# Two thirds of a condition projection on VectorE instead of TensorE, in a two-block model on one core

## The chip, the core and the metric

The kernel runs on one core of one Trainium2 chip. The metric is the device time of one execution in microseconds (us). The engines are named as in the profile: PE is TensorE's matrix multiply and PEld its weight load, DVE is VectorE, ACT is ScalarE, POOL is GpSimd, SP is the engine whose queue issues most of the transfers.

## The reference, cut to what matters

The model has two parts. The first is two layers of a hybrid mixer (two attentions and a gated short convolution) and a feed-forward part, on 256 tokens of 1024 features. The second takes the result through an mLSTM mixer, a mixture of experts, a retention mixer and again a mixture of experts; its norms are modulated by two conditions, `c` for the 256 tokens and `c_ctx` for a context of 256 tokens more:

```python
for i in range(DEPTH):                     # DEPTH is 2
    mod_l = jnp.split(c_lat @ ada_w[i] + ada_b[i], N_MOD, axis=-1)   # ada_w[i]: [1024, 6144]
    mod_c = jnp.split(c_con @ ada_w[i] + ada_b[i], N_MOD, axis=-1)
    h_lat = modulate(rmsnorm(x, norm_mix_g[i]), mod_l[0], mod_l[1])
    h_ctx = modulate(rmsnorm(ctx, norm_mix_g[i]), mod_c[0], mod_c[1])
    ...
```

`c_lat` and `c_con` are silu of the two conditions. The condition projection depends on nothing that the first part computes, only its results are needed in the second part. In the last layer the context's results are needed for the mixer alone.

## The kernel before

All weights are float32 and come through one stream of chunks, 128 partitions by 2048 columns (1 MB), in the order of their use; SP issues their loads (`load`, L409). Four tiles take the raw chunks in turn. A chunk of a projection is split into two parts for TensorE: ACT copies its high part (`split`, L421), DVE forms its low part as raw minus high (L422), in two halves of 1024 columns each. Three pairs of tiles hold the parts. A product of two float32 operands is then three matmuls (`mm3`, L473 to L475: high by high, low by high, high by low). A column chunk of a projection is 48 such matmuls of 256 columns.

The plan of the stream (`stream_plan`) puts the 48 chunks of the condition projection (`"ada"`, 24 for each layer of the second part) into the first part of the model: 4 at the end of each mixer and of each feed-forward part (16 in all; `layer_norm` emits them, L887), and 32 spread over the rest of the first part, one about every third or fourth chunk. An `ada` chunk isn't split: `ada_chunk` (L494) multiplies it in 8 float32 matmuls by the two conditions, which stand as narrow columns in `csil`, over four groups of array columns; the four chunks of a group are added into `part` (ACT L500 for the first, DVE L502 for the others), and `ada_finish` turns a group with two matmuls (L510) and adds the bias (DVE L514) into `modc`, where every gain, shift and gate of the second part is read from. That makes 12 groups.

`parts(key)` is how every product gets its chunk: it first calls `run_ada`, which emits the condition chunks that stand next in the stream, and then `get`, which starts loads so that two chunks stand ready behind the one in use. A scheduler sets the order of each engine's instructions ahead of the run; every engine then runs its own list in order, so an instruction that waits holds up all behind it.

The first part's mixer (`mixer`) takes its projections in the order cq, ck, cv, aq, akv (L778 to L802), works through 8 tiles of two heads in `attention_pair` (scores L736 on PE, L740 to L750 on DVE, exp L752 and L753 on ACT, L758 to L760 on DVE, transposes L763 on PE, then the product with the values, L767 and L768), while PE also works on the convolution's projections (bc, bh, bb), then through 12 gate chunks with 6 branch chunks, and 4 output chunks. The feed-forward part (`ffn`) has 22 pairs of column tiles (g) and 11 chunks of the way down (d). `layer_norm` stands behind each; the rows for its gain and bias are loaded into two tiles with the tag `bc`.

Of the kernel before, what the change touches and what calls it, by code (L numbers as in the profile page):

```python
# [18 lines left out]
P = 128  # L19
T = 256  # L20
# [19 lines left out]
ADA_END = 4  # L40
NG = 4
# halves of chunks whose low parts GpSimd forms, VectorE being busy at that time
# [65 lines left out]
def stream_plan():  # L108
# [10 lines left out]
    # the ada chunks: some where the two blocks' parts meet, the others in between  # L119
    ada = [("ada", i, n) for i in range(LAYERS) for n in range(24)]  # L120
    spread = len(ada) - ADA_END * len(ends)
    free = [k for k in range(9, n1 - 4) if not any(e - 4 <= k <= e for e in ends)]
    mids = [free[len(free) * k // spread] for k in range(spread)]
    out = []
    for k, key in enumerate(plan):
        out.append(key)
        for _ in range(ADA_END * (k in ends) + mids.count(k)):
            out.append(ada.pop(0))
    assert not ada
# [16 lines left out]
def _pack(w):  # L146
    """[K, n] -> [P, (K / P, n)]"""
    k, n = w.shape
    return np.ascontiguousarray(w.reshape(k // P, P, n).transpose(1, 0, 2)).reshape(P, -1)


def _pack2(w):
    """[K, 2 n] -> [P, (2, K / P, n)]: a column half after the other."""
    n = w.shape[1] // 2
    return np.concatenate([_pack(w[:, :n]), _pack(w[:, n:])], axis=1)


def _chunk(key, x):
# [20 lines left out]
    if kind == "dn":  # L179
        return _pack(x["w_ffn_down"][key[1]][key[2] * 256 : key[2] * 256 + 256])  # L180
    if kind == "ada":
        return _pack(x["ada_w_2"][key[1]][:, key[2] * 256 : key[2] * 256 + 256])
# [26 lines left out]
# ---------------------------------------------------------------- small operands  # L209
# [58 lines left out]
def _rows(x):  # L268
# [6 lines left out]
    return np.stack(rows + [misc]).astype(np.float32)  # L275


def _constants():
# [23 lines left out]
    # distances of the keys (partition) from the queries: of the context backwards, of the latent stream backwards,  # L302
    # of the latent stream forwards (those past the key's tile first), of the context forwards
# [13 lines left out]
def kernel(  # L317
# [18 lines left out]
    # ------------------------------------------------------------ pools  # L336
# [17 lines left out]
    def bank(pool, tag, one=None):  # L354
        """The next of four banks in turn; one: False for one of the first three, True for the fourth."""
# [14 lines left out]
    # ------------------------------------------------------------ resident operands  # L370
# [21 lines left out]
    # ------------------------------------------------------------ weight stream  # L392
# [5 lines left out]
    def load(key, mid=None):  # L398
        """Start the load of the next chunk of the stream; mid: called between its halves."""
# [15 lines left out]
    def split(key, w, pair, half=None):  # L415
        """The float32r parts (hi, lo) of every 1024 columns of a chunk (or of one half), in the tiles of pair."""
# [9 lines left out]
    def load_parts(key):  # L426
        """Load the next chunk, as float32r parts."""
# [8 lines left out]
    def get(key, ahead=AHEAD):  # L436
        """The chunk of a key; the ones after it are started first."""
        while len(ready) < 1 + ahead and state["i"] < len(plan) and plan[state["i"]][0] != "moe":
            k = plan[state["i"]]
            ready.append((k, load(k) if k[0] == "ada" else load_parts(k)))  # L440
# [8 lines left out]
    def run_ada(end=False, rest=False):  # L449
        """The next ada chunks, and the ends of the last ones. At an end also the chunks behind those that are  # L450
        ready, their ends follow some chunks later; rest: all that is left."""
# [3 lines left out]
        while True:  # L455
            key = ready[0][0] if ready else None
            if key is None or key[0] != "ada":
# [13 lines left out]
    def mm3(o, st, mv, first, last):  # L471
        """o (+)= st^T mv in float32 from the parts (hi, lo) of both."""
# [4 lines left out]
    def warm(n):  # L477
        """Keep the tensor engine's clock up while a chain of short operations runs elsewhere."""
# [4 lines left out]
    # ------------------------------------------------------------ modulation  # L483
# [21 lines left out]

    def ada_finish():
# [16 lines left out]
    # ------------------------------------------------------------ small helpers  # L523
    def rsqrt(v, n, tag="nw"):
        """v ** -0.5 of a [P, n] tile by Newton's iteration."""
# [30 lines left out]
    def parts_of(pair, at, full):  # L556
        """pair[at] = parts of a float32 SBUF operand."""
# [10 lines left out]
    def evac_parts(ps, kp, dst, col0, gain, bias, direct=()):  # L568
        """dst (pair) [:, ko, col0 + 0:256] = parts of ps[:, k] * gain[ko] + bias[ko], ko = 2 kp + k."""
# [16 lines left out]
    def squares(ss, s, c, src, route=None):  # L586
        """ss [P, 2, streams, 4]: sums of squares of a column chunk, by token; route: whose scratch to use."""
# [8 lines left out]
    def rms_early(ss, n):  # L596
        """rms_rstd's share of all sums but the last."""
# [5 lines left out]
    def rms_rstd(ss, n, early=None):  # L603
        """1 / rms of every token, [P, n], from the sums of squares of some chunks [P, n, chunks]."""
# [4 lines left out]
    def diagonals(rs, n, pool, tag, bufs=1):  # L609
        """[P, n, P]: diagonal matrices of the columns of rs."""  # L610
# [5 lines left out]
    def normed(src, dg, dst, col0, gain, shift, bank=ax_bank, direct=()):  # L616
        """dst (pair) [:, ko, col0 + 0:256] = parts of (scaled src)^T * gain[ko] + shift[ko]; dg: by token tile."""
# [1559 lines left out]
```

## Time and profile before

| | |
|---|---|
| three runs | 2396.39 us median, 2392.59 to 2402.55 |
| profiled execution: span from the first to the last instruction | 2391.9 us (its own whole time is not given apart; the fastest run is 0.7 above the span, the median 4.5) |
| first part of the model | about 0 to 945 us of the span |
| PE busy | 2182.5 us (91%), 16939 instructions |
| DVE busy | 1093.7 us (46%), 2176 instructions |
| ACT busy | 737.6 us (31%) |
| chain of work that ended last | PE 65%, transfers 27%, DVE 6%, ACT 2% |
| granted TensorE clock over the span | 0.952 |

The page gives each engine's busy time over the whole span, and its share in 40 slices of the span, about 60 us each. An engine's average hides stages: the first part of the model is the first 16 slices, and the two mixtures of experts wait mostly for their weights. So the views used below are cut to stretches of the first part: 60 to 265 us is about the first layer's mixer (from its attention on), 265 to 460 its feed-forward part, 460 to 740 the second layer's mixer, 740 to 945 its feed-forward part. In the views, a row for a group of instructions has line, engine, operation, tiles and shapes, then the count, the busy time, the mean of one in ns, and the idle time ahead of them with what ended it.

### The profile page before, as it was taken

To read this page: it belongs to the slowest core of one execution; us is meant where nothing else is said; L and a number is where in the kernel's file an instruction comes from. 1 tells how busy PE (TensorE), PEld (TensorE's weight loads), DVE (VectorE), ACT (ScalarE), POOL (GpSimd) and SP (SyncE) were. 2 spreads that over 40 slices of the span, in tenths; PEclk is the share of its full clock that TensorE was granted. 3 is DMA by queue.
4 is the path that set the end of the run, shared out by engine and by line. 5 is a ranking of instruction groups with operands and counts; after the bars stand their busy time and mean duration, and the time that the engine had idled before them with its cause. 6 is when DMAs were issued, how large, how long until landed. Compare 5 with 4: busy or idle time off the path is not lost.

```text
span 2391.9 us, 39835 instructions
## 1 busy us (share of the span) xinstructions
PE 2182.5 (91%) x16939; PEld 1626.3 (68%) x16939; DVE 1093.7 (46%) x2176; ACT 737.6 (31%) x1353; POOL 76.3 (3%) x112
## 2 busy tenths in 40 slices
PE   8999999999999999999999999887899998766666
PEld 8799989897998998798885533222599874322222
DVE  5755744567567546765842222121573632010102
ACT  4543444345445444546521100000342521000000
POOL 0000000000000001201200000000110100000000
PEclk9999999999999999999999999999999999676777
DMA  7355666663557565122269999999743699999997
GB/s 297 129 189 229 257 240 233 240 221 122 211 216 299 212 236 186 71 106 71 81 272 360 408 372 421 421 421 421 298 152 107 229 365 420 421 421 421 421 420 294
DMA packets 92048, 652.40 MB, mean 273 GB/s; under 512 B 10336, under 2 KB 10592, under 8 KB 13920
## 3 DMA queue, kind: packets, MB, share of 16 engines
q1 hardware_dynamic: 89424, 641.61, 68.0%
q10 hardware_dynamic: 2448, 8.26, 1.0%
q8 instruction: 133, 2.18, 0.4%
q14 instruction: 43, 0.35, 0.0%
HBM read 648.78 MB, written 1.05 MB: 272 GB/s over the span
## 4 chain that ended last, share of the span: by engine, by line
PE 65%; DMA 27%; DVE 6%; ACT 2%; issue 1%; POOL 0%; ACTq 0%; SPq 0%; DVEq 0%; POOLq 0%
DMA w<-in_ws_dram 27%; PE mm L473 13%; PE mm L474 13%; PE mm L475 13%; PE mm L1726 5%; PE mm L1795 2%; PE mm L1220 2%; PE ax L473 2%; PE mm L494 2%; PE ax L475 2%; PE ax L1608 2%; PE ax L474 2%; PE ax L736 1%; PE ax L1815 1%; PE ax L623 1%
## 5 line engine op out<-in xcount | busy, mean ns | idle before, releaser
L422 DVE TENSOR_TENSOR lo<-w,hi 128x1024 fp32r<-128x1024 f32 x337 | 409.7, 1234 | 296.3 <-ACT hi L421 295.7
L421 ACT ACTIVATE hi<-w 128x1024 fp32r<-128x1024 f32 x343 | 352.3, 1053 | 462.8 <-PE mm L474 210.7
L1726 PE MATMUL mm<-w,xsT 128*32 128x256 f32 (+1 forms) x3072 | 404.2, 520 | 94.0 <-DMA w<-in_ws_dram 92.3
L473 PE MATMUL mm<-xTh,hi 128*128 128x256 f32 x1488 | 418.9, 282 | 6.5 <-ACT xTh L559 6.5
L474 PE MATMUL mm<-xTl,hi 128*128 128x256 f32 x1488 | 416.8, 280 | 1.5 <-DVE xTl L560 0.8
L475 PE MATMUL mm<-xTh,lo 128*128 128x256 f32 x1488 | 416.5, 280 | 0.0
L1726 PEld LDWEIGHTS mm<-w,xsT 128*32 128x32 f32 (+1 forms) x3072 | 141.8, 132 | 344.5 <-issue 169.2
L473 PEld LDWEIGHTS mm<-xTh,hi 128*128 128x128 f32 x1488 | 281.6, 190 | 21.4 <-issue 12.8
L474 PEld LDWEIGHTS mm<-xTl,hi 128*128 128x128 f32 x1488 | 281.2, 189 | 5.0 <-issue 2.3
L475 PEld LDWEIGHTS mm<-xTh,lo 128*128 128x128 f32 x1488 | 280.7, 189 | 2.9 <-issue 2.7
L1795 PE MATMUL mm<-w,xt 128*64 128x512 f32 x480 | 108.3, 596 | 9.6 <-DVE xt L1765 7.1
L1746 ACT ACTIVATE xt<-mm 128x512 f32<-128x512 f32 x16 | 9.6, 597 | 326.4 <-PE mm L1726 326.4
L1747 DVE TENSOR_TENSOR ag<-ag,mm 128x256 f32<-128x256 f32 x16 | 6.7, 421 | 225.3 <-PE mm L1726 193.8
L1746 ACT ACTIVATE ag<-mm 128x256 f32<-128x256 f32 x16 | 6.1, 383 | 334.7 <-PE mm L1726 334.7
L1747 DVE TENSOR_TENSOR xt<-xt,mm 128x512 f32<-128x512 f32 x16 | 11.0, 687 | 207.9 <-PE mm L1726 207.9
L1795 PE MATMUL mm<-w,ag 128*32 128x256 f32 x960 | 78.3, 469 | 29.1 <-DMA w<-in_ws_dram 22.5
L1784 DVE TENSOR_TENSOR yg<-mm,bc 32x512 f32<-32x512 f32 x60 | 41.2, 687 | 110.7 <-PE mm L1795 110.0
L1795 PEld LDWEIGHTS mm<-w,xt 128*64 128x64 f32 x480 | 33.4, 137 | 73.1 <-issue 55.7
L1795 PEld LDWEIGHTS mm<-w,ag 128*32 128x32 f32 x960 | 31.4, 130 | 70.3 <-DMA w<-in_ws_dram 39.1
L473 PE MATMUL mm<-hi,hTh 128*128 128x256 f32 x256 | 71.8, 281 | 2.9 <-ACT row L1435 2.9
L474 PE MATMUL mm<-lo,hTh 128*128 128x256 f32 x256 | 71.6, 280 | 0.0
L475 PE MATMUL mm<-hi,hTl 128*128 128x256 f32 x256 | 71.6, 280 | 0.0
(483 smaller groups left out, 4056.4 us busy)
## 6 DMA issues: line engine op xcount, KB each, us to landing
w<-in_ws_dram SPq DMA_DIRECT2D x607, 1024.0 KB, 10.9
bc<-in_rows_dram ACTq DMA_DIRECT2D x10, 512.0 KB, 8.7
w<-in_ws_dram SPq DMA_DIRECT2D x3, 512.0 KB, 4.1
xf<-in_x_feat_dram SPq DMA_DIRECT2D x4, 256.0 KB, 5.9
X<-in_x_tok_dram SPq DMA_DIRECT2D x1, 1024.0 KB, 12.8
C<-in_c_tok_dram ACTq DMA_DIRECT2D x1, 1024.0 KB, 8.8
dist<-in_csr_dram ACTq DMA_DIRECT2D x1, 640.0 KB, 3.7
out_dram<-X SPq DMA_DIRECT2D x2, 256.0 KB, 2.6
```

Source lines behind the costliest of these rows:

```text
L421: S.activation(hi[at], w[at], AF.Copy)
L422: (G if (key, k) in POOL_LO else V).tensor_tensor(lo[at], w[at], hi[at].bitcast(F32), op=ALU.subtract)
L473: TE.matmul(o, st[0], mv[0], start=first, stop=False)
L474: TE.matmul(o, st[0], mv[1], start=False, stop=False)
L475: TE.matmul(o, st[1], mv[0], start=False, stop=last)
L494: TE.matmul(ps[g * 32 : g * 32 + 32, :256], c, w[:, 2 * g + k, :], start=(k == 0), stop=(k == 1), tile_position=(0, g * 32),)
L623: TE.matmul(ps[:, k, tt * P : tt * P + P], src[:, tt, ko * P : ko * P + P], dg[tt], start=True, stop=True)
L1220: TE.matmul(pg[:, k, :N], self.src[:, tt, ko * P : ko * P + P], PT[:, tt, :], start=(tt == 0), stop=(tt == 1),)
L1608: TE.matmul(pa[:, k, :], E[d, jt][:, columns_of(d, jt, it * P, it * P + P)], v[h // 4][:, jt, h % 4, :], start=(jt == js[0]), stop=(jt == ...
L1726: end = TE.matmul(ps[g * M : g * M + M, :hw], st, w[:, k, g * hw : g * hw + hw], start=(c == 0 and k == 0), stop=(c == 3 and k == 1), tile ...
L1784: V.tensor_tensor(yg[s][32 * q : 32 * q + 32, at], pd[r : r + 32, :w], gate[r : r + 32, at], op=ALU.mult)
L1795: TE.matmul(pd[g * M : g * M + M, :hw], hidden(kt), w[:, k, g * hw : g * hw + hw], start=(kt == 0), stop=(kt == KO - 1), tile_position=(0, ...
```

## The change

The 32 condition chunks that are spread over the first part get a new kind, `"adv"`, and go to DVE. Such a chunk is stored transposed: a partition holds two of the chunk's 256 output features, with all 1024 inputs of each along its row. `adv_chunk` multiplies a row by a condition that is copied into all partitions (`cbc`, half of silu is made by the factor 0.5) and sums the product along the row, in one DVE instruction per feature and condition, 128x1024 each; the sum goes straight into `modc`, and the products into a `bc` tile that nobody reads. One small DVE instruction then adds the bias. A chunk has 4 such long instructions where both conditions are needed (16 chunks) and 2 where one is enough (the second layer's features from the ninth chunk on, 16 chunks): 96 in all, and 32 small ones. The 16 chunks at the layer norms stay on PE as before, with 4 of the 12 groups; they now are chunks 8 to 23 of the first layer, and the DVE chunks are the first layer's 0 to 7 and all 24 of the second. The DVE chunks stand between the first layer's chunk bc1 and the second layer's g6, 8 in the first mixer (32 long instructions), 11 in its feed-forward part (38), 11 in the second mixer (22) and 2 behind it (4).

New at the start are two transfers of 512 KB on SP's queue (a condition into all partitions), and for each a tanh on ACT and a product on DVE, both 128x1024 (L731 and L732 of the changed kernel). For the place that `cbc` takes, three tiles of the mixer go into others: `cv` into two tiles with the tag `th`, `mrh` into the tiles of `lg` and `ex`, which grow from 384 to 512 columns.

```diff
+ADV_FROM = 12
...
-    ada = [("ada", i, n) for i in range(LAYERS) for n in range(24)]
-    spread = len(ada) - ADA_END * len(ends)
-    free = [k for k in range(9, n1 - 4) if not any(e - 4 <= k <= e for e in ends)]
-    mids = [free[len(free) * k // spread] for k in range(spread)]
+    at_end = [("ada", 0, n) for n in range(24 - ADA_END * len(ends), 24)]
+    between = [("adv", i, n) for i in range(LAYERS) for n in range(24) if ("ada", i, n) not in at_end]
+    stop = plan.index(("gu", LAYERS - 1, 6))
+    free = [k for k in range(ADV_FROM, stop) if not any(e - 4 <= k <= e for e in ends)]
+    mids = [free[len(free) * k // len(between)] for k in range(len(between))]
...
+    if kind == "adv":
+        w = x["ada_w_2"][key[1]][:, key[2] * 256 : key[2] * 256 + 256]
+        return np.ascontiguousarray(w.T.reshape(2, P, D).transpose(1, 0, 2)).reshape(P, -1)
...
     def run_ada(end=False, rest=False):
...
             key = ready[0][0] if ready else None
+            if key is not None and key[0] == "adv":
+                adv_chunk(key[1], key[2])
+                continue
...
+    def adv_chunk(i, n):
+        w = get(("adv", i, n)).rearrange("p (f k) -> p f k", f=2)
+        ns = 1 if i == LAYERS - 1 and n >= 8 else 2
+        at = slice(2 * n, 2 * n + 2)
+        for s in range(ns):
+            for f in range(2):
+                junk = tmp([P, D], "bc", bufs=2, pool=state["adap"])
+                V.scalar_tensor_tensor(
+                    junk, w[:, f, :], 0.5, state["cbc"][:, s, :], op0=ALU.mult, op1=ALU.mult,
+                    accum_out=modc[:, i, 2 * n + f, s : s + 1],
+                )
+        bias = pcol("adab", 48 * i + 2 * n, 2)[:, :, None].to_broadcast([P, 2, ns])
+        V.tensor_tensor(modc[:, i, at, :ns], modc[:, i, at, :ns], bias, op=ALU.add)
...
+                G.memset(modc, 0.0)
+                cbc = state["cbc"]
+                cz = tmp([P, D], "bc", bufs=2, pool=b1), tmp([P, D], "bc", bufs=2, pool=b1)
+                for k in range(2):
+                    S.activation(cz[k], cbc[:, k, :], AF.Tanh, scale=0.5)
+                    V.scalar_tensor_tensor(cbc[:, k, :], cz[k], 1.0, cbc[:, k, :], op0=ALU.add, op1=ALU.mult)
...
-                cv = mx.tile([P, 2, 512], F32, tag="cv", name=nm("cv"))
+                cv = [tmp([P, 2, T], "th", bufs=2, pool=mx) for _ in range(2)]
...
+                    for k in range(2):
+                        nc.sync.dma_start(state["cbc"][:, k, :], row_bc(11 + k))
                     conditions()
...
-                mrh = mx.tile([P, KO, T], F32R, tag="mrh", name=nm("mrh"))
+                mrh = [tmp([P, 2, T], t, F32R, bufs=2, pool=mx) for t in ("lg", "lg", "ex", "ex")]
```

On PE, this is what stands between a branch product of the first mixer (`mm_1589`, `mm_1603` after) and the next gate's product (`mm_1642`, `mm_1638`), where the fourth condition chunk stood; before:

```order
L474 MATMUL mm_1589<-yl_1121,hi_1402 128x256
L475 MATMUL mm_1589<-yh_1120,lo_1403 128x256
L494 MATMUL mm_1624<-w_1528,csil 32x256 x8
L473 MATMUL mm_1642<-xTh_84,hi_1533 128x256
L474 MATMUL mm_1642<-xTl_85,hi_1533 128x256
L475 MATMUL mm_1642<-xTh_84,lo_1534 128x256
```

and after:

```order
L484 MATMUL mm_1603<-yl_1141,hi_1461 128x256
L485 MATMUL mm_1603<-yh_1140,lo_1462 128x256
L483 MATMUL mm_1638<-xTh_84,hi_1544 128x256
L484 MATMUL mm_1638<-xTl_85,hi_1544 128x256
L485 MATMUL mm_1638<-xTh_84,lo_1545 128x256
```

The 8 matmuls of the condition chunk are gone, and the two products follow each other directly.

On DVE, this is where the first mixer's attention sets in, around the values of the second attention (L802, L842 after); `lg_758` holds the scores of the second tile of two heads. Before:

```order
L422 TENSOR_TENSOR lo_1126<-w_1123,hi_1125 128x1024 x2
L793 COPY aq_113<-mm_600 128x256
L802 COPY aq_113<-mm_626 128x256
L740 SCALAR_TENSOR_TENSOR lg_687<-csa_89,ax_680 128x384
L740 SCALAR_TENSOR_TENSOR lg_708<-csa_89,ax_681 128x384
L745 TENSOR_REDUCE mx_689<-lg_687 128x1
```

and after:

```order
L429 TENSOR_TENSOR lo_615<-w_612,hi_614 128x1024 x2
L833 COPY aq_117<-mm_620 128x256
L524 SCALAR_TENSOR_TENSOR bc_1391,modc<-w_1268,cbc 128x1024
L524 SCALAR_TENSOR_TENSOR bc_1393,modc<-w_1268,cbc 128x1024
L524 SCALAR_TENSOR_TENSOR bc_1395,modc<-w_1268,cbc 128x1024
L524 SCALAR_TENSOR_TENSOR bc_1397,modc<-w_1268,cbc 128x1024
L529 TENSOR_TENSOR modc<-modc,prm 128x4
L842 COPY aq_117<-mm_646 128x256
L429 TENSOR_TENSOR lo_1146<-w_1143,hi_1145 128x1024 x2
L778 SCALAR_TENSOR_TENSOR lg_758<-csa_93,ax_751 128x384
```

The first tile's scores have moved ahead of this place, and the four long instructions of the first DVE chunk stand together between the two copies, ahead of the next low parts and of the second tile's scores.

On SP's queue, behind the first weights, before:

```order
L782 DMA csa_89<-in_csa_dram 128x768
L782 DMA sk<-in_rows_dram 128x32
L782 DMA X<-in_x_tok_dram 128x2048
L409 DMA w_250<-in_ws_dram 128x2048
L409 DMA w_308<-in_ws_dram 128x2048
```

and after:

```order
L820 DMA csa_93<-in_csa_dram 128x768
L820 DMA sk<-in_rows_dram 128x32
L820 DMA X<-in_x_tok_dram 128x2048
L822 DMA cbc<-in_rows_dram 128x1024 x2
L416 DMA w_264<-in_ws_dram 128x2048
L416 DMA w_322<-in_ws_dram 128x2048
```

The two copies of the conditions stand ahead of the chunks cv0 and cv1.

## Rows read from the trace of the kernel before

**Rows 1.** The page, its busy shares in 40 slices of the span (tenths), PE and DVE.

```profile
PE   8999999999999999999999999887899998766666
DVE  5755744567567546765842222121573632010102
```

**Rows 2.** Stretches of the first part: PE, PEld, DVE, ACT, POOL busy, clock, DMA share, GB/s.

```profile
60.00:265.00 205.00, 203.21 (x1678) 183.04 (x1678) 128.24 (x240) 95.03 (x175) 0.22 (x2) 1.00 0.50 187
265.00:460.00 195.00, 193.84 (x1528) 175.47 (x1527) 104.92 (x151) 87.53 (x121) 0.00 (x0) 1.00 0.66 243
460.00:740.00 280.00, 277.47 (x2333) 251.24 (x2331) 178.44 (x327) 126.39 (x214) 0.12 (x1) 1.00 0.55 201
740.00:945.00 205.00, 204.88 (x1589) 184.47 (x1590) 116.19 (x171) 93.69 (x138) 0.00 (x0) 1.00 0.64 237
```

**Rows 3.** Waits of PE, 20 to 960 us: total, times, longest.

```profile
PE ax L763 <- DVE ex L759: 1.6, 2, 1.4
```

**Rows 4.** Waits of DVE, 20 to 960 us.

```profile
DVE lo L422 <- ACT hi L421: 254.4, 118, 6.2
```

**Rows 5.** PE in order of time: start, duration, instruction; around one condition chunk.

```profile
205.45 0.28 PE L475 MATMUL mm<-yh,lo 128*128 128x256 f32 x1
205.66 1.07 PE L494 MATMUL mm<-w,csil 128*32 128x256 f32 x16
206.66 0.38 PE L473 MATMUL mm<-xTh,hi 128*128 128x256 f32 x1
206.88 0.28 PE L474 MATMUL mm<-xTl,hi 128*128 128x256 f32 x1
207.00 0.28 PE L475 MATMUL mm<-xTh,lo 128*128 128x256 f32 x1
```

**Rows 6.** PE in order of time, around the end of a group.

```profile
170.52 0.28 PE L475 MATMUL mm<-yh,lo 128*128 128x256 f32 x1
170.64 0.51 PE L510 MATMUL mm<-cst,part 128*128 128x8 f32 x4
171.00 0.36 PE L473 MATMUL mm<-xTh,hi 128*128 128x256 f32 x1
171.20 0.28 PE L474 MATMUL mm<-xTl,hi 128*128 128x256 f32 x1
```

**Rows 7.** DVE by line, whole span.

```profile
L422 DVE TENSOR_TENSOR lo<-w,hi 128x1024 fp32r<-128x1024 f32 x337 | 409.7, 1234 | 296.3 <-ACT hi L421 295.7
...
L917 DVE SCALAR_TENSOR_TENSOR X<-res,nwy,bc 128x1024 f32<-128x1024 f32 x8 | 9.9, 1277 | 0.0
...
L1398 DVE TENSOR_TENSOR_SCAN row<-row 8x512 f32<-8x512 f32 x1 | 1.2, 1212 | 0.7 <-POOL row L1397 0.7
...
L514 DVE TENSOR_TENSOR modc<-mm,prm 128x16 f32<-128x16 f32 x12 | 2.0, 170 | 12.2 <-PE mm L510 12.1
```

**Rows 8.** DVE in order of time, from the second attention's values on.

```profile
63.20 0.42 DVE L802 COPY aq<-mm 128x256 f32<-128x256 f32 x1 [4.06 <-PE mm L475]
64.05 1.02 DVE L740 SCALAR_TENSOR_TENSOR lg<-csa,ax 128x384 f32<-128x384 f32 x2 [0.43 <-PE ax L736]
...
65.18 0.41 DVE L746 TENSOR_REDUCE mx<-lg 128x1 f32<-128x256 f32 x1
```

**Rows 9.** ACT in order of time: a tile's exp, and a high part that waited for its load.

```profile
27.99 2.01 ACT L421 ACTIVATE hi<-w 128x1024 fp32r<-128x1024 f32 x2 [0.50 <-DMA w<-in_ws_dram]
...
66.52 0.40 ACT L752 ACTIVATE ex<-lg,mx 128x128 f32<-128x128 f32 x1
66.83 0.19 ACT L752 ACTIVATION_READ_ACCUMULATOR ex<-lg,mx 128x1 f32 x1
66.92 0.49 ACT L753 ACTIVATE ex<-lg,mx 128x256 f32<-128x256 f32 x1
```

**Rows 10.** Transfers by what they fill: KB each, median us from issue to landing.

```profile
w<-in_ws_dram SPq DMA_DIRECT2D x607, 1024.0 KB, 10.9
bc<-in_rows_dram ACTq DMA_DIRECT2D x10, 512.0 KB, 8.7
```

More of the change, by code (lines that the diff above doesn't have):

```diff
@@ L126, in stream_plan @@
         out.append(key)
-        for _ in range(ADA_END * (k in ends) + mids.count(k)):
-            out.append(ada.pop(0))
-    assert not ada
+        for _ in range(ADA_END * (k in ends)):
+            out.append(at_end.pop(0))
+        for _ in range(mids.count(k)):
+            out.append(between.pop(0))
+    assert not at_end and not between
     return out
@@ L274, in _rows @@
     misc[16:32] = x["ret_decay_logit_2"].reshape(-1)
-    return np.stack(rows + [misc]).astype(np.float32)
+    return np.stack(rows + [misc, x["c_2"][0], x["c_ctx_2"]]).astype(np.float32)
 def _constants():
@@ L439, in get @@
             k = plan[state["i"]]
-            ready.append((k, load(k) if k[0] == "ada" else load_parts(k)))
+            ready.append((k, load(k) if k[0] in ("ada", "adv") else load_parts(k)))
         if not ready:
@@ L663, in first_block @@
             xT = part_pair(b1, [P, KO, T], "xT")
+            esv = es.enter_context(ExitStack())
+            vp = esv.enter_context(tc.tile_pool(name="vp", bufs=1, side="right", reuse_waits="tile"))
+            state["cbc"] = vp.tile([P, 2, D], F32, tag="cbc", name="cbc")
             def begin(l, mx):
@@ L712, in pair_feat, with tile_of @@
                 return ps.rearrange("p (m t) -> p m t", m=2)
+            def tile_of(a, ko):
+                return a[ko // 2][:, ko % 2] if isinstance(a, list) else a[:, ko]
             def pair_tok(key, src=None, split=False):
@@ L722, in pair_tok @@
                             half[tt],
-                            [a[:, ko, tt * P : tt * P + P] for a in (src or xT)],
+                            [tile_of(a, ko)[:, tt * P : tt * P + P] for a in (src or xT)],
                             [a[:, ko % 4, :] for a in w[ko // 4]],
@@ L738, in attention_pair @@
                 for s, (r, sc) in enumerate(zip(rows, scs)):
-                    lg = tmp([P, 384], "lg", bufs=2, pool=state["mx"])
+                    lg = tmp([P, 512], "lg", bufs=2, pool=state["mx"])[:, :384]
                     V.scalar_tensor_tensor(lg, con(table), float(slopes[s]), sc[:, :384], op0=ALU.mult, op1=ALU.add)
@@ L750, in attention_pair @@
                         V.tensor_scalar(mx, mx, sink[s], -1.0, op0=ALU.max, op1=ALU.mult)
-                    ex = tmp([P, 384], "ex", bufs=2, pool=state["mx"])
+                    ex = tmp([P, 512], "ex", bufs=2, pool=state["mx"])[:, :384]
                     S.activation(ex[:, 0:P], lg[:, 0:P], AF.Exp, bias=mx[:, 0:1], accum_out=sm[:, 0:1])
@@ L786, in mixer @@
                 for c in range(2):
-                    V.tensor_copy(cv[:, :, c * 256 : c * 256 + 256], pair_tok(("in", l, "cv", c)))
+                    V.tensor_copy(cv[c], pair_tok(("in", l, "cv", c)))
                 for c in range(2):
@@ L810, in mixer @@
                         cq[:, m, :], ck[:, m, :],
-                        cv[:, :, 128 * m : 128 * m + 64], cv[:, :, 128 * m + 64 : 128 * m + 128],
+                        *(cv[m // 2][:, :, at : at + 64] for at in (128 * (m % 2), 128 * (m % 2) + 64)),
                         "moba", sl, None, yc, m,
@@ L865, in mixer @@
                         if n == 2:
-                            S.activation(mrh[at], mrf[at], AF.Copy, scale=0.5)
+                            S.activation(mrh[c], mrf[at], AF.Copy, scale=0.5)
                             V.scalar_tensor_tensor(
-                                mrl[at], mrf[at], 0.5, mrh[at].bitcast(F32), op0=ALU.mult, op1=ALU.subtract
+                                mrl[at], mrf[at], 0.5, mrh[c].bitcast(F32), op0=ALU.mult, op1=ALU.subtract
                             )
@@ L944, in ffn @@
                             S.dma_start(pre["rows"][k], row_bc(4 * l + 2 + k))
+                        esv.close()
                         context(b1)
```

## The prediction

> **What bounds the kernel now.** I read the page first, then the chain of work that ended last, then the stretches of the first part, then the waits, and single stretches in order of time. In the 40 slices [rows 1] PE is at 9 tenths in nearly all of the first 16, where the change is made; DVE is at 4 to 7 there. Cut to stretches [rows 2], PE is busy 879.4 of the 885 us from 60 to 945 us, at a granted clock of 1.00, the upper level (2.4 GHz), throughout. A busy PE need not be a full one, since matmuls overlap in the record, so I look at starts: one matmul of 256 columns follows the other after 0.12 us (206.88 to 207.00) [rows 5], and PE's longest wait there for the softmax on DVE is 1.4 us [rows 3]. PE sets the pace of this part. DVE is busy 128, 105, 178 and 116 us of the four stretches [rows 2], and its largest wait is for ACT's high parts, 254 us in 118 waits, 6.2 at most [rows 4]: it forms a low part as soon as the pair of tiles comes free, and then has nothing to do. These gaps are where the change puts its work.
>
> **What goes.** A condition chunk on PE: the last matmul before it starts at 205.45, the second after it at 206.88; without it two steps of 0.115 would lie between, so it costs 1.43 - 0.23 = 1.20 us [rows 5], more than its 1.07 us of busy time, since the weight load behind it is not hidden. 32 chunks: 38.4 us. The end of a group in the same way: 170.52 to 171.20 less 0.23, 0.45 us [rows 6]; 8 of 12 go: 3.6 us. All of these stand between products that PE runs without a gap, so I count them whole: **42.0 us**. The 16 chunks at the layer norms stay, at no difference.
>
> **What comes on DVE.** 96 long instructions. The nearest row is the scalar-tensor-tensor over two float32 operands in SBUF, 128x1024: 1.28 us [rows 7]; it doesn't sum. No DVE row sums along a row on the side. From below it can hardly be quicker than that row, since it reads the same and writes the same. From above I take the running sum: 512 elements in 1.21 us [rows 7], so 2.42 for 1024. Between them ACT's summing exp stands nearest: its read of the sum is a record of 0.19 us, and the next instruction starts 0.09 us after that record's start [rows 9]. I take 1.28 plus 0.09, **1.37 us**. Add 0.17 for a bias instruction, as one takes now [rows 7], and take off 24 additions to `part`, at about the 0.42 us of a 256-column copy [rows 8].
>
> Is there room? First mixer: 128.2 + 32 x 1.37 + 8 x 0.17 - 6 x 0.42 = 170.9 of 205 us (83%). First feed-forward part: 104.9 + 38 x 1.37 + 11 x 0.17 - 8 x 0.42 = 155.5 of 195 (80%). Second mixer: 178.4 + 22 x 1.37 + 1.9 - 8 x 0.42 = 207 of 280 (74%). There is room on average, so the sum of DVE's work costs nothing; what can cost is its order.
>
> **Where a low part is late.** A pair of part tiles comes free three chunks ahead, two chunks of PE (48 x 0.115 = 5.5 us each, so 11 us) before its next contents are due; ACT and DVE need about 1.05 + 2 x 1.2 = 3.5 us of that. The slack of some 7.5 us covers a block of four long instructions, 5.5 us. In the gate and feed-forward stretches I therefore take nothing, with 0 to 3 us for the two chunks right behind each layer norm, where DVE also updates X (1.28 us an instruction [rows 7]); taken: 2.
>
> **Where the softmax is late.** In the attention, DVE's results are waited for within microseconds. The first DVE chunk stands as a block between the copies of the second attention's keys and values, ahead of the second tile's scores (the order shown above). From the first copy on DVE needs 0.42 + 4 x 1.37 + 0.2 + 0.42, two low parts 2.4, scores 0.55, a low part of the tile 0.4, maxima 0.7, ACT's two exps 0.9, reciprocal and scaling 0.8: 12.3 us until that tile's transposes can start. PE has the values' product ahead of them, 4.5 us (DVE's 0.42 for the first copy and its wait of 4.06 until the second [rows 8]), 32 matmuls of the convolution (3.7 us) and some 14 small ones of the first tile, about 2: 10.2 us. It waits 2 us, and longer by whatever the DVE chunk's own load is late: the transfer is issued only when a raw tile comes free and takes a median 10.9 us [rows 10], so 0 to 5 more. I take 4 for it. The next chunk's four instructions are spread over the second attention, one ahead of each tile's maxima: 0 to 5, taken 2. The second mixer has three chunks of two in its attention, blocks of 2.7 us: 0 to 8, taken 3.
>
> **At the start.** The two new transfers stand ahead of cv0 and cv1 on SP's queue, 1 MB more in a stretch where the stream is still catching up (a high part waits 0.50 us for its load at 27.99 [rows 9]). ACT's two tanh (1.05 us each, as a high part) and DVE's two products (1.28) stand ahead of cv0's parts on those queues, 2.6 us on DVE. The chunks have two others ahead of them on PE; 0 to 5, taken 1. The tiles that share places cost nothing by themselves: `cv` is read by the first attention before the convolution writes its tile, and `mrh` is written long after the last `lg` and `ex`.
>
> **The sum.** -42.0 + 2 + 4 + 2 + 3 + 1 = -30 us on the profiled span of 2391.9; the median of the runs is 4.5 above that span, so 2396.4 - 30 = **2366.4 us**. The second part follows the first through its data, and its waits for weights begin only after the first routing, so it moves as a whole. With every stall at its lower end the time is 2354.4, with all at the upper end (3 + 7 + 5 + 8 + 5 = 28) 2382.4.
>
> **Rivals.** *The softmax takes it all back.* The same blocks, with DVE at 80% and more, make each attention tile late: 16 tiles by 2.5 us each would be 40 us, against the 16 to 42 gained. For it: PE already waits once for a softmax [rows 3]. Against: the order is laid out with the long instructions in it, and PE has convolution matmuls between. About 2392 us, 0.13.
>
> *The freed time isn't PE's.* If the stretches went by the parts' round of tiles (PE frees, ACT, DVE, PE), removing PE work would lengthen its idle only. Against it: PE idles 5.6 of 885 us [rows 2]. About 2394 us, 0.04.
>
> *The summing form runs at half rate.* At the running sum's 2.42 us [rows 7] the first mixer needs 128.2 + 77.4 + 1.4 - 2.5 = 204.5 us of DVE and the feed-forward part 104.9 + 92.0 + 1.9 - 3.4 = 195.4: DVE is full in both, and becomes the bound there. Its waits for ACT and PE don't vanish (77 and 90 us in the two stretches now); a quarter kept makes them 224 and 218 us, 42 longer, while the second mixer and what follows still save 13 x 1.2 = 16. That gives 2396.4 + 26 = 2422 us. It decides from about 1.85 us an instruction, where 128.2 + 32 x 1.85 - 1.1 + 19 = 205. For it: a sum carried along has that rate in one row. Against: the row at 1.28 us reads two float32 operands at the full rate [rows 7]. 0.08.
>
> The Trainium skill has a rule for this rival ("Vector Engine (DVE) Microarchitecture Reference", section "Points that are easy to get wrong"): a scalar-tensor-tensor with two sources in SBUF that aren't bf16 halves its throughput, because both read ports are taken and none is left for the accumulator. By that rule alone the instruction would take about 2.5 us (an estimate from that page's factor and the row of 1.28), and the time would be the third rival's; the trace speaks against the factor for the form without a sum, and has no row for the form with one.
>
> **The numbers.** 0.73 for the forecast with its bounds, 0.13, 0.04 and 0.08 for the rivals, 0.02 for something else that is slower. The measurement tells 0.5%, 12 us, from no change. Of the first rival a quarter still lies over 12 us below: faster 0.76, same 0.14, slower 0.10. The range goes from 2350 (no stall at all, less the 3.8 us by which the fastest run lies under the median) to 2397, which takes in the first two rivals and leaves out the third.
>
> **What would show it.** Right: no `csil` matmul outside the layer norms (256 records instead of 768), 96 DVE records near 1.37 us, the end of the first part about 30 us earlier, PE idle up by some 12 us, most of it ahead of transposes from 60 to 140 us. Wrong: long instructions of 1.9 us and more; PE waits for low parts in the gate or feed-forward stretches; the second part longer than before.

## The result, and the profile after

| | before | after |
|---|---|---|
| median of the runs (lowest to highest) | 2394.49 us (2392.36 to 2402.55) | 2357.91 us (2354.59 to 2364.67) |
| ratio to before | | 0.985, interval 0.9826 to 0.9874 |
| span of the profiled execution | 2391.9 us | 2355.1 us |

The change makes the kernel 36.6 us faster, 1.5%. The forecast of 2366.4 was 8.5 us too slow; the result lies in its range and on its side. Of the 8.5, 1.9 are the median of before, 2394.5 here and 2396.4 where the forecast began, and 6.6 are its terms (36.6 against 30).

From the page of the kernel after: engines, and busy shares in 40 slices.

```profile
span 2355.1 us, 38884 instructions
PE 2143.8 (91%) x16395; PEld 1605.9 (68%) x16395; DVE 1195.9 (51%) x2370; ACT 738.5 (31%) x1347; POOL 77.0 (3%) x113
...
PE   8999999999999999999999999887899998666665
...
DVE  6788887678767556947642312122563732010102
```

PE's busy time falls from 2182.5 to 2143.8 us, by 38.7, and the span by 36.8: nearly every microsecond taken from PE came off the end. DVE is 102 us busier, PE's slices still stand at 9 tenths through the first part, and DVE's, 4 to 7 before [rows 1], are now 5 to 8.

The same stretches as [rows 2], after: PE, PEld, DVE, ACT, POOL busy, clock, DMA share, GB/s.

```profile
60.00:265.00 205.00, 202.63 (x1630) 184.59 (x1630) 163.18 (x314) 95.52 (x170) 0.20 (x2) 1.00 0.54 201
265.00:460.00 195.00, 192.13 (x1425) 177.14 (x1424) 153.29 (x237) 88.13 (x120) 0.00 (x0) 0.99 0.72 270
460.00:740.00 280.00, 277.53 (x2285) 258.65 (x2284) 211.76 (x375) 136.95 (x229) 0.12 (x1) 1.00 0.59 219
```

DVE stands at 163 of 205 and 153 of 195 us, below the 171 and 155.5 that were forecast. The third stretch, 212 us against 207, compares less well, since the program is 19 us ahead when it begins. PE is still all but full.

Waits of PE, then of DVE, from 20 to 930 us, after: total, times, longest.

```profile
PE mm L504 <- DMA w<-in_ws_dram: 2.4, 2, 2.0
PE mm L485 <- DVE lo L429: 1.8, 4, 0.8
...
PE ax L801 <- DVE ex L797: 0.6, 2, 0.3
```

```profile
DVE lo L429 <- ACT hi L428: 133.6, 79, 5.8
DVE bc L524 <- DMA w<-in_ws_dram: 26.8, 13, 3.8
```

PE waits 1.8 us for low parts and 0.6 us for the softmax, which was 1.6 us before [rows 3]. The new work went into DVE's wait for high parts, which fell from 254 [rows 4] to 134 us. DVE even waits 26.8 us for the loads of its own chunks, and PE doesn't notice.

The products and the sums, one group each: duration in ns (least, median, greatest), first and last start.

```profile
L524 DVE SCALAR_TENSOR_TENSOR bc<-w,cbc x96: 1214/1219/1227, 59.3 to 742.0; 128x1024 f32<-128x1024 f32 x96
L524 DVE DVE_READ_ACCUMULATOR bc<-w,cbc x96: 80/83/90, 60.4 to 743.1; 128x1 f32 x96
```

**By stages.** At the end of each layer norm ACT centers the tokens; the first of these records marks a stage in the timeline. The first and the fourth of them, before and then after:

```profile
267.54 1.15 ACT L901 ACTIVATE res<-res,nm 128x1024 f32<-128x1024 f32 x1
944.90 2.19 ACT L901 ACTIVATE res<-res,nm 128x1024 f32<-128x1024 f32 x2 [2.40 <-DVE nm L898]
```

```profile
258.93 1.15 ACT L941 ACTIVATE res<-res,nm 128x1024 f32<-128x1024 f32 x1
908.48 2.19 ACT L941 ACTIVATE res<-res,nm 128x1024 f32<-128x1024 f32 x2 [2.40 <-DVE nm L938]
```

So the first part ends 36.4 us earlier, and the rest of the span takes 2391.9 - 944.9 = 1447.0 us before and 2355.1 - 908.5 = 1446.6 after. The same markers in every kernel that ran (us):

| kernel | first mixer | first feed-forward | second mixer | second feed-forward | rest |
|---|---|---|---|---|---|
| before | 267.5 | 205.4 | 264.7 | 207.2 | 1447.0 |
| after | 258.9 | 194.6 | 256.7 | 198.3 | 1446.6 |
| after, once more | 260.0 | 194.5 | 256.3 | 197.4 | 1446.8 |
| before, chunks not multiplied | 254.7 | 192.7 | 255.0 | 198.4 | 1449.8 |
| after, no products on DVE | 259.6 | 192.7 | 255.6 | 198.2 | 1445.6 |
| after, products twice | 275.7 | 212.7 | 256.2 | 198.2 | 1444.9 |
| before, places shared | 269.5 | 205.3 | 264.1 | 206.7 | 1448.7 |
| after, conditions late | 256.8 | 194.4 | 254.4 | 197.4 | 1449.9 |
| after, 2 chunks at each norm on PE | 260.5 | 194.4 | 258.1 | 197.5 | 1450.4 |
| after, none on PE | 267.2 | 200.1 | 263.7 | 197.5 | 1449.8 |

Two traces of one kernel agree within 1.1 us a stage. The rest, which no edit touches, differs by up to 5.5 us between kernels, and the runs of one kernel spread over 10 us (2354.59 to 2364.67 after).

**A second measure.** Stages of different kernels can differ by some microseconds that no edit explains, because PE's own pace varies. In all these traces a 256-column matmul in a row of its like follows the one before it, nearly everywhere, either after about 0.113 us or after about 0.118 us. Here are the same 12 us of the gate chunks in the kernel after, in its first and in its second trace:

```profile
222.00:234.00 12.00, 12.00 (x108) 12.00 (x108) 6.86 (x9) 5.58 (x8) 0.00 (x0) 1.00 0.59 220
222.00:234.00 12.00, 12.00 (x104) 12.00 (x104) 6.36 (x8) 5.08 (x7) 0.00 (x0) 1.00 0.66 237
```

PE is busy all the time at a granted clock of 1.00, and starts 108 matmuls in the one and 104 in the other. The program is the same, so it doesn't settle the spacing by itself; what does is open. One spacing can last long: without the products on DVE it is the longer one from 165 to 255 us. A mixer has some 1670 such steps, so up to 7.5 us of it hang on this. Added up over the four stages, the time above 0.113 us a step is 11.8 us before, 7.8 after (7.1 once more), 9.1 with the chunks not multiplied, 13.4 without the products and 3.6 with the conditions late. Below, a difference "at equal spacing" has this time taken off both kernels.

### The profile page after: what moved, and what is told of

It reads as the page before. It is cut to its first block, busy times and chain, and to the rows that moved or that the text cites. A ratio compares the mean times of both kernels' runs of the same rounds, so it can differ in the third digit from the quotient of the medians.

```text
span 2355.1 us, 38884 instructions
## 1 busy us (share of the span) xinstructions
PE 2143.8 (91%) x16395; PEld 1605.9 (68%) x16395; DVE 1195.9 (51%) x2370; ACT 738.5 (31%) x1347; POOL 77.0 (3%) x113
## 4 chain that ended last, share of the span: by engine, by line
PE 59%; DMA 30%; DVE 8%; ACT 2%; issue 1%; POOL 0%; ACTq 0%; SPq 0%; DVEq 0%; POOLq 0%
DMA w<-in_ws_dram 30%; PE mm L484 12%; PE mm L485 12%; PE mm L483 12%; PE mm L1767 5%; PE mm L1836 2%; DVE lo L429 2%; PE mm L1261 2%; PE ax L1649 2%; PE ax L485 1%; PE ax L484 1%; PE ax L483 1%; PE ax L774 1%; PE ax L805 1%; PE ax L648 1%
## 5 line engine op out<-in xcount | busy, mean ns | idle before, releaser
L524 DVE SCALAR_TENSOR_TENSOR bc<-w,cbc 128x1024 f32<-128x1024 f32 x96 | 114.7, 1220 | 26.8 <-DMA w<-in_ws_dram 26.8
L1825 DVE TENSOR_TENSOR yg<-mm,yg 32x256 f32<-32x256 f32 x60 | 25.2, 420 | 99.1 <-PE mm L1836 93.7
## 6 DMA issues: line engine op xcount, KB each, us to landing
cbc<-in_rows_dram SPq DMA_DIRECT2D x2, 512.0 KB, 11.3
```

What stands on the lines that cost most here:

```text
L524: V.scalar_tensor_tensor(junk, w[:, f, :], 0.5, state["cbc"][:, s, :], op0=ALU.mult, op1=ALU.mult, accum_out=modc[:, i, 2 * n + f, s : s + 1],
L1825: V.tensor_tensor(yg[s][32 * q : 32 * q + 32, at], pd[r : r + 32, :w], gate[r : r + 32, at], op=ALU.mult)
```

## The experiments

The theory: PE sets the pace of the first part, its removed work comes off whole, and DVE takes the products into idle time at a small price in late results. The rivals: the products give most of it back; the sharing of places or the new start does something of its own; the chunks at the layer norms matter too.

**The removal alone.** In the kernel before, the 32 chunks between the norms are loaded and not multiplied.

```diff
+    ENDS = [(0, n) for n in (8, 9, 10, 11, 20, 21, 22, 23)] + [(1, n) for n in (9, 10, 11, 12, 20, 21, 22, 23)]
     def ada_chunk(i, n):
         w = get(("ada", i, n)).rearrange("p (k n) -> p k n", k=KO)
+        if (i, n) not in ENDS:
+            return
+        i, n = 0, ENDS.index((i, n))
```

> The kernel before, with its 32 condition chunks between the norms loaded as before but not multiplied (their 256 matmuls on PE, their additions on DVE and 8 of the 12 group ends are left out, so their modulation values stay zero). It asks what this work costs PE by itself, with nothing put in its place. If a chunk costs 1.20 us of PE's path and a group's end 0.45, as read from the starts around them, it is 42 us faster than before: about 2352. If only the busy time counts (1.07 and less, or part of it hidden), 36 us or less: 2358 and up. If something other than PE sets the pace of the first part, nothing: 2394.

Measured: 2353.74 us (2351.12 to 2362.75), ratio 0.9842 [0.9823, 0.9861], 39.7 below the median of before measured beside it (2393.43). The four stages of the first part are 44.0 us shorter, the rest 2.8 longer. At equal spacing it is 41.4. The removed work was on the path, whole; the change reaches all but 3 us of this by medians, and all but 7.6 by stages.

**The products alone.** In the kernel after, the loop of the 96 long instructions is left out; the loads, the start and the bias additions stay.

```diff
-        for s in range(ns):
-            for f in range(2):
-                junk = tmp([P, D], "bc", bufs=2, pool=state["adap"])
-                V.scalar_tensor_tensor(
...
-                )
```

> The changed kernel without the 96 long products on VectorE (the chunks are loaded and only the bias is added, so these modulation values lack the product). Everything else of the change stays: the tiles that share places, the transfers and tanh at the start, the plan. If VectorE's work is hidden but for the few low parts and the norm whose last chunk came late, it is 2 to 5 us faster than the changed kernel, 2353 to 2356. If the long products cost what the prediction took for them (12 us), 2346. If they cost nothing and the 5.6 us that the stages lack to 42 come from the other parts of the change, no difference: 2358.

Measured: 2353.44 us (2348.85 to 2361.38), ratio 0.9838 [0.9817, 0.9859]: 4.5 us below after by medians, though the spreads overlap. By stages the products cost 2.4 us: 1.9 in the first feed-forward part and 1.1 in the second mixer, while the first mixer, with a third of them, is no longer for them (258.9 against 259.6). At equal spacing they cost 2.1, 1.1, 4.7 and 0.1 us in the four stages, 8.0 in all. So their price is some 2 to 8 us, and these runs don't narrow it. From the stretches of this kernel, the columns as above:

```profile
60.00:265.00 205.00, 203.83 (x1628) 186.65 (x1628) 128.57 (x240) 94.98 (x169) 0.21 (x2) 1.00 0.54 200
265.00:460.00 195.00, 193.31 (x1458) 179.00 (x1456) 111.02 (x153) 91.09 (x126) 0.00 (x0) 1.00 0.73 274
```

Here DVE has 129 and 111 us of work in these stretches, and with the products 163 and 153. The 77 us between them are hidden but for 1 to 3.

**The products twice.** Each is done two times in a row, to the same place.

```diff
-        for s in range(ns):
+        for s in [s for s in range(ns) for _ in range(2)]:
```

> The changed kernel with every long product issued twice in a row (same operands, same result), 192 instead of 96: what an instruction of 2.4 us would have done. By VectorE's busy time (163 of 205 and 153 of 195 us in the first two stretches, plus 37 and 45), VectorE is full in both; with a quarter of its idle time kept they end 11 and 15 us later: about 2384, 26 us over the changed kernel. If blocks count by the slack of a pair of part tiles (7.5 us against a block of 10), each of the 16 long blocks makes PE wait 2 to 3 us: 2390 to 2406. If the work stays hidden, 2358.

Measured: 2393.50 us (2389.39 to 2400.72), ratio to before 1.0005 [0.9994, 1.0016]: 35.6 us above after by medians and 34.3 by stages, the whole gain gone. Stretches and PE's waits (20 to 930 us):

```profile
60.00:262.00 202.00, 187.83 (x1438) 170.92 (x1437) 180.89 (x340) 85.61 (x159) 0.10 (x1) 0.97 0.48 177
262.00:475.00 213.00, 201.90 (x1484) 187.94 (x1483) 198.60 (x320) 91.11 (x125) 0.10 (x1) 0.96 0.66 245
```

```profile
PE mm L483 <- ACT hi L428: 9.5, 3, 4.4
PE mm L485 <- DVE lo L429: 7.8, 8, 3.4
PE ax L801 <- DVE ex L797: 3.4, 3, 2.7
```

With 181 of 202 us (90%) and 199 of 213 (93%), DVE sets the pace: the first mixer is 16.8 us longer than after and the first feed-forward part 18.1, the second mixer, with 22 products more, 0.5 shorter. PE now idles for high and low parts, and the granted clock falls to 0.97 and 0.96 of the upper level. These shares are of stretches that have grown. What DVE was asked for is what it had, 163 and 153 us, and once more what the first set had added, 35 and 42: 198 of 205 us and 196 of 195, by the windows used for the kernel after. So the room that the prediction counted is real: products that cost 2 to 8 us while they fit cost 34 to 36 once DVE is full.

**The shared places alone.** The kernel before with `cv` in two tiles of `th`, `mrh` in those of `lg` and `ex`, and these at 512 columns.

```diff
-                cv = mx.tile([P, 2, 512], F32, tag="cv", name=nm("cv"))
+                cv = [tmp([P, 2, T], "th", bufs=2, pool=mx) for _ in range(2)]
...
-                mrh = mx.tile([P, KO, T], F32R, tag="mrh", name=nm("mrh"))
+                mrh = [tmp([P, 2, T], t, F32R, bufs=2, pool=mx) for t in ("lg", "lg", "ex", "ex")]
```

> The kernel before with the shared places alone: the values of the first attention in two tiles of the gates' tag, the merged branches' high parts in the tiles of the softmax, which grow to 512 columns. Nothing else. If sharing places costs and gains nothing, no difference: 2394, within 3. If the attention's earlier start in the changed kernel's order comes from the sharing and is part of the gain, up to 5 us faster: 2389. If a shared tile makes its next writer wait, slower by a few us.

Measured: 2396.57 us (2393.04 to 2404.16), ratio 1.0015 [1.0003, 1.0028], 0.15% above before. Its first mixer is 2.0 us longer, the three other stages not at all. The 2 us arise before any shared tile is used. The timeline's start in this kernel, and the same high part in the kernel before:

```profile
0.80 0.41 ACTq L643 DMA_DIRECT2D C<-in_c_tok_dram  x1
...
7.42 1.06 ACT L421 ACTIVATE hi<-w 128x1024 fp32r<-128x1024 f32 x1 [4.90 <-DMA w<-in_ws_dram]
```

```profile
4.90 1.06 ACT L421 ACTIVATE hi<-w 128x1024 fp32r<-128x1024 f32 x1 [2.82 <-DMA w<-in_ws_dram]
```

The scheduler put the context's transfer ahead of everything on ACT's queue, and the first weights land 2.5 us later. Neither the kernel before nor the one after has that. Sharing itself costs nothing that can be seen.

**The new start alone.** The kernel after, with the two copies of the conditions, their tanh and their products (now `condition_rows`) behind the copies of `cv`.

```diff
+            def condition_rows():
+                cbc = state["cbc"]
...
                     V.tensor_copy(cv[c], pair_tok(("in", l, "cv", c)))
+                if l == 0:
+                    condition_rows()
...
-                    for k in range(2):
-                        nc.sync.dma_start(state["cbc"][:, k, :], row_bc(11 + k))
```

> The changed kernel with the two condition rows loaded, and their tanh and product made, behind the values of the first attention (after chunk cv1) instead of behind the first queries; nothing else. In the changed kernel the step from the second copy of keys to the first copy of values takes 12.8 us, in the kernel before 11.3 to 11.6, in the one without the long products 13.4. If the new loads and the two steps on ACT and VectorE ahead of cv0 are that difference, the step goes back to about 11.3 and the time to 2356. If it is only variation of the start, no difference: 2358.

Measured: 2354.78 us (2353.06 to 2358.32), ratio to before 0.9842 [0.9823, 0.986]; 3.1 below after by medians, a difference that these runs don't tell from none, since their spreads overlap. At the place itself, DVE in order of time, after:

```profile
26.02 0.69 DVE L825 COPY qk<-mm 128x512 f32<-128x512 f32 x1 [2.76 <-PE mm L485]
26.63 2.35 DVE L732 SCALAR_TENSOR_TENSOR cbc<-bc,cbc 128x1024 f32<-128x1024 f32 x2
...
38.82 0.68 DVE L827 COPY th<-mm 128x512 f32<-128x512 f32 x1
```

and with the conditions late:

```profile
26.65 0.69 DVE L827 COPY qk<-mm 128x512 f32<-128x512 f32 x1 [2.76 <-PE mm L485]
...
37.53 0.69 DVE L829 COPY th<-mm 128x512 f32<-128x512 f32 x1 [0.74 <-PE mm L485]
```

From the first copy of the keys to the first of the values it is 12.8 us after (12.8 in its second trace too) and 10.9 here; before it is 11.3. That looks like a price of the new start, but PE loses nothing there. After, its stretch from 26 to 39 us, and what it does in the middle of it; then the same matmuls with the conditions late:

```profile
26.00:39.00 13.00, 13.00 (x108) 12.29 (x108) 12.10 (x15) 7.93 (x12) 0.00 (x0) 1.00 0.97 379
```

```profile
31.35 0.48 PE L774 MATMUL ax<-qk 64*128 64x128 f32 x2
...
32.08 0.92 PE L774 MATMUL ax<-qk 64*128 64x128 f32 x6
```

```profile
62.31 0.93 PE L778 MATMUL ax<-qk 64*128 64x128 f32 x8
```

PE is busy throughout. The step is longer because the first tile's scores, 8 small matmuls and 1.4 us, stand in it; with the conditions late they come 30 us later, and in the kernel before at 63.09. The first mixer is 2.2 us shorter with the conditions late, but the second mixer, which has no part in the start, is 2.3 shorter too. At equal spacing the whole first part is 1.4 us shorter (1.8 against the second trace of after), 0.6 of it in the first mixer. So the new start costs 0 to 2 us, and that its two products on DVE (2.35 us) hold PE up isn't shown.

**The chunks at the norms.** Two experiments move them to DVE as well: `ADA_END` 2 leaves 2 chunks at each norm on PE, and 0 none (128 and 160 products on DVE instead of 96).

```diff
-ADA_END = 4
+ADA_END = 2
```

> The changed kernel with two condition chunks on PE at each norm instead of four: 8 more go to VectorE, 128 long products instead of 96. If PE at the norms only fills its wait for the norm's chain, the 8 chunks give back little there (0 to 5 us, the late fourth chunk at the second norm among it), and VectorE, which has some 30 us of room in each of the first three stretches, hides the 32 new products: 2353 to 2358. If the blocks already cost PE by their number, each of 40 chunks a little, 2360 or more. If the tensor engine's clock falls at the norms without the fill, some us more.

> The changed kernel with all 48 condition chunks on VectorE: 160 long products, none on PE. VectorE's busy time then comes to about 190 of 199, 180 of 194 and 240 of 257 us in the first three stretches, between the changed kernel and the one with every product twice, which lost 17 and 18 us in the first two. Expected 10 to 25 us slower than the changed kernel, 2368 to 2383, less what PE saves at the norms (0 to 10). If room alone decides, no loss: 2350 to 2358.

Measured: 2363.58 us (2358.85 to 2369.63), ratio to before 0.9881 [0.9858, 0.9904], and 2378.38 us (2372.22 to 2380.3), 0.9928 [0.9905, 0.9951]: 5.7 and 20.5 us above after by medians, 2.0 and 20.0 by stages, although PE has 8 and 16 chunks less. PE's waits with 2 chunks, then with none, and two stretches of the latter:

```profile
PE ax L648 <- DVE sg L945: 10.8, 3, 4.1
```

```profile
PE ax L648 <- DVE sg L945: 17.5, 3, 5.9
PE ax L801 <- DVE ex L797: 9.4, 3, 5.2
PE mm L485 <- DVE lo L429: 2.5, 3, 1.1
```

```profile
265.00:270.00 5.00, 0.00 (x0) 0.00 (x0) 4.72 (x17) 3.92 (x4) 0.00 (x0) 0.91 0.87 320
270.00:275.00 5.00, 4.50 (x21) 4.53 (x22) 1.76 (x6) 1.32 (x3) 0.00 (x0) 0.50 0.88 339
```

In the kernel after, PE has no wait for the norm's `sg` among its longest; with two chunks less it waits 10.8 us in 3 norms, with none 17.5. In the first norm without chunks PE stands still for the five microseconds from 265 on, and the next five run at a granted clock of 0.50, the lower level (1.2 GHz). The norm's 32 transposes, after and then without chunks:

```profile
261.68 3.81 PE L648 MATMUL ax<-sg,res 128*128 128x128 f32 x32
```

```profile
270.50 6.39 PE L648 MATMUL ax<-sg,res 128*128 128x128 f32 x32 [5.81 <-DVE sg L945]
```

From the last product ahead of a norm to the first behind it PE takes 8.8, 13.4 and 8.8 us in the first three norms after, and 12.2, 13.7 and 12.4 without chunks, some 7 us more. So a chunk that costs PE 1.20 us between products [rows 5] fills a wait for DVE at a norm, and taking it away gains nothing. The largest loss lies elsewhere: the first mixer is 8.3 us longer without chunks, nearly all of it ahead of its norm. DVE is at 176 of 205 us there (86%), and PE's largest wait in the two mixers is for the softmax, 9.4 us. The first feed-forward part, with DVE at 178 of 195 us (91%), is 5.5 longer, of which the norm ahead of it takes 3.4 and PE's spacing 2.7. DVE and PE at the second attention's second tile, with no chunk on PE:

```profile
69.45 1.23 DVE L524 SCALAR_TENSOR_TENSOR bc<-w,cbc 128x1024 f32<-128x1024 f32 x1 [4.61 <-DMA w<-in_ws_dram]
```

```profile
76.82 0.30 PE L801 MATMUL ax<-cst,ex 128*128 128x128 f32 x1 [3.92 <-DVE ex L797]
```

DVE waits 4.6 us for the load of its own chunk, with the values' copy and the second tile's scores behind it in its list, and PE's transposes wait 3.9. With two chunks at each norm the loss, 2.0 us by stages, is too small for these runs to tell it from none.

**The kernel after once more**, to see how far its stages repeat.

> The changed kernel once more, for a second trace: how far the lengths of the four stretches between the norms, and the spacing of matmuls within them, vary from one execution to the next. If they are the program's, each stretch is within 1 us of the first trace (258.9, 194.6, 256.7 and 198.3 us). If a spacing of 0.113 against 0.117 us is chance, stretches move by up to 3%, and differences of some us between single traces mean nothing.

Measured: 2358.25 us (2356.8 to 2359.69), ratio 0.9853 [0.9827, 0.9878]. Its stages are within 1.1 us of the first trace, and inside them the spacing changes from 0.113 to 0.118 us at other places.

## Why the prediction was right, and which terms were off

**PE as the bound, and the removal of 42.0 us: right.** Taking the chunks out alone gives 39.7 us by medians, 44.0 by stages and 41.4 at equal spacing. The rival that the freed time isn't PE's is refuted by the same run.

**The long instruction at 1.37 us: too dear.** A record is 1.22 us, and one starts 1.14 us after the other. The attention's first block in the kernel after, DVE in order of time:

```profile
58.92 0.42 DVE L833 COPY aq<-mm 128x256 f32<-128x256 f32 x1
...
60.40 0.08 DVE L524 DVE_READ_ACCUMULATOR bc<-w,cbc 128x1 f32 x1
60.40 1.22 DVE L524 SCALAR_TENSOR_TENSOR bc<-w,cbc 128x1024 f32<-128x1024 f32 x1
61.54 0.08 DVE L524 DVE_READ_ACCUMULATOR bc<-w,cbc 128x1 f32 x1
61.54 1.22 DVE L524 SCALAR_TENSOR_TENSOR bc<-w,cbc 128x1024 f32<-128x1024 f32 x1
...
70.54 0.35 DVE L798 TENSOR_SCALAR ex<-ex,rd 128x256 f32<-128x256 f32 x1
```

The read of the sum lies beside the next instruction, whose start it doesn't delay visibly. So the lower bound of 1.28, which the prediction took from the form that doesn't sum, was still above the truth, and the running sum's 2.42 no guide. The third rival (half rate, 2422 us) is refuted. So is, for this form, the rule of the Trainium skill that the prediction set beside it ("Vector Engine (DVE) Microarchitecture Reference", section "Points that are easy to get wrong"): two float32 sources in SBUF and a sum on the side should have halved the rate, and this case's 96 records at 1.22 us show the rate of the plain subtraction (1.23 us [rows 7]).

**The stalls, 2 + 4 + 2 + 3 = 11 us: too dear by 3 to 9.** Leaving the products out gains 2.4 us by stages, 4.5 by medians and 8.0 at equal spacing. The largest piece, 4 us for the second attention's first tiles, didn't come. DVE's side was forecast well: from the copy of the keys until the second tile is scaled it needed 12.3 us by the prediction and 12.0 in the trace (58.92 to 70.89, the first and the last row above). PE's cover was forecast too short, at 10.2 us. PE in order of time, the first tile's transposes and then the second's:

```profile
63.15 0.52 PE L801 MATMUL ax<-cst,ex 128*128 128x128 f32 x3
...
71.22 0.27 PE L801 MATMUL ax<-cst,ex 128*128 128x128 f32 x1
```

The values' product covers 4.2 us, as forecast (4.5), but the small matmuls and the convolution's behind it take 8.1 us where 5.7 were counted: the convolution's 32 are there and take their 3.7, the small ones some 4.4 instead of 2. PE comes to the second tile 12.3 us after the copy and doesn't wait, with 0.3 us to spare. The margin is thin: with 160 products and a late load this very tile cost PE 3.9 us. At 96 products all of PE's waits for the softmax come to 0.6 us, so the rival that the softmax takes everything back is refuted there.

**Where a cost of the products can be seen** is the norm behind the first feed-forward part, which the prediction had at 0 to 3 us for late low parts. There it is a late load. PE in order of time, and the stretch behind it:

```profile
454.38 1.85 PE L504 MATMUL mm<-w,csil 128*32 128x256 f32 x16 [2.00 <-DMA w<-in_ws_dram]
```

```profile
455.00:460.00 5.00, 5.00 (x38) 3.94 (x31) 2.40 (x13) 0.68 (x1) 0.00 (x0) 0.71 1.02 387
```

PE stands 2.0 us for the fourth chunk at the norm, the granted clock of the next stretch is 0.71, between its two levels, and that chunk's records take 1.85 us where one takes 1.07 at the upper level [rows 5]. Without the products the same wait is 0.8 us and the clock stays at 1.00 there. That the products hold a raw tile longer, and so delay the load, is argued, not shown.

**The start, taken at 1 us,** cost 0 to 2. **The shared places at 0: right.** **DVE's busy time** rose by 102 us where 127 was forecast, by the price of the long instruction. **The lower end of the time, 2354.4,** takes every stall at nothing, though by the prediction's own sum PE waits 12.3 - 10.2 = 2 us in the second attention at least; it should have been 2356.4.

Of the marks named ahead, 256 `csil` records, 96 long ones and an earlier end of the first part (36 us instead of 30) held. The long records were 1.22 us, not near 1.37. PE's idle time from 60 us to the end of the first part rose from 5.6 us (of 885) to 7.9 (of 848), not by some 12, and little of it lies ahead of transposes. Waits for low parts, named as a sign of being wrong, do appear in the gate and feed-forward stretches, at 1.8 us in all.

By terms, then: the removal of 42.0 lies among its measures (39.7 to 44.0). The 12 us of stalls and start were between 2 and 10, so they were too dear and are part of the miss of 6.6. How large a part stays open. At equal spacing 41.4 go and 9.0 come back, 32.4 in all, 2.4 more than the forecast. The other 4.0 of the traces' difference are PE's spacing, 11.8 us before and 7.8 after: the prediction had no term for it, and the runs don't show whether the change has a part in it. Direction and mechanism are the prediction's; how near the number came is partly luck.

## What to carry to other kernels

When one engine sets the pace and another waits in regular gaps, work moved over can be nearly free: here at 80% of the stretch, for 2 to 8 us of 42. When it asked for all of the stretch it cost the whole gain. In between the share alone doesn't tell: a mixer at 86% lost 8 us, with late softmax results among its waits, while a feed-forward part at 91% lost next to nothing of its own. So count room by stretch, look at what waits for the late results, and test it by doubling the moved work. What the engine is relieved of counts only where it had no wait to fill: a chunk between products was worth 1.2 us, while the chunks at the norms covered waits, and moving them gained nothing. Before pricing a late result, count everything that the waiting engine still has in front of it, small matmuls too. And before giving a few microseconds of a trace to an edit, see whether the engine ran at the same pace in both, and whether it waited at all.

## What the runs showed that was not expected

A DVE product with a row sum costs no more than one without: starts 1.14 us apart for 128x1024 float32, with the 0.08 us read of the sum beside the next one. PE's 256-column matmuls come at one of two spacings, 0.113 or 0.118 us, at the same granted clock, and the same program changes between them at different places in two traces. And a pause of PE at a norm costs more than its length: after five idle microseconds the granted clock was 0.50 in the next five, and 0.71 after a pause of 2 us. What sets the spacing, and what makes the untouched second part differ by up to 5.5 us between kernels, stays open.
